# An encoder layer's feed-forward entry: one norm product of the up-projection a matmul group later, two operand steps tied behind others

## The chip, the core and the metric

The kernel runs on one core of a Trainium2 chip. The metric is the device time of one execution in microseconds (us). Engines are named as the profile names them: PE (TensorE), ACT (ScalarE), DVE (VectorE), POOL (GpSimd), SP (the engine that issues most transfers).

## What is computed

One layer of a streaming encoder over 1072 tokens (16 meta tokens and 1024 frames of a new stream, 32 frames of a running one) at width 1024: a norm, one input projection for a convolution group and for attention, an output projection with a residual, and the part that matters here:

```python
def conv_ffn(x, gate_past, g, w_up, dw_w, dw_b, w_down):
    h = rmsnorm(x, g)
    u = h @ w_up
    gate, up = u[..., :D_FF], u[..., D_FF:]
    gate_ext = jnp.concatenate([gate_past, gate], axis=1)
    y = jax.nn.silu(depthwise_causal_conv(gate_ext, dw_w, dw_b)) * up
    return x + y @ w_down, gate_ext[:, -(FFN_CONV_WIDTH - 1):]
```

`rmsnorm(x, g)` is `x / sqrt(mean(x*x) + eps) * g`, and `D_FF` is 2816: 22 row groups f of 128 channels, each with a gate row and an up row.

## The kernel before

Data lie feature by token: 128 channels on the partitions, tokens along the free dimension. A product of two float32 operands is made of three matmuls on high and low parts: high by high, high by low, low by high (`mm3`, L261). A high part is a rounded copy that ACT makes, a low part the difference, made by DVE (`hilo` for weights, L1327; `gsplit` for x times the norm's weight, L311).

Tokens come in three blocks at the end of the convolution group. `conv_half` (L1262) adds the convolution group's product to x, sums the squares of x into `rb` on POOL (L309), and makes the high and low parts `bh` and `bl` of x times the norm's weight (L312, L313). Its columns m are taken in the order 0, 1, 4, 5, 6, 7, 2, 3, so that the last low part of block 2 is that of m = 3.

The norm's scale is not applied to x but to the rows that come out of the up-projection. `rms2` (L1282) makes it for a block in three steps of `rms_steps` (L269). The first is PE's product of `rb` with ones (L280), which gives the sums over channels per token, then the mean plus eps on DVE (L283, called the variance here), its power of -1/2 on POOL (L287) and three small refining instructions on DVE (L288, L289, L291). The second is three diagonal matrices on ACT (L295). The third is PE's product of ones with the diagonals (L301), the scale broadcast to all partitions, which ACT copies to `rbg`.

The feed-forward begins with f = 0 and f = 1 in plain form. `group(f, u, p, c)` (L1676) is one product of 24 matmuls: u = 0 is the gate row and u = 1 the up row, and p and c choose one of four pieces of 264 tokens from token 16 on (268 for the first of the gate row, with its left edge). The pieces p = 0 read blocks 0 and 1 of x; group 2 of a row, the piece p = 1 and c = 0, begins at token 544 and is the first that reads block 2, which begins at token 720. The loop at L1705 makes the four groups of the gate row of f = 0, called groups 0 to 3 here. The last block's norm (`last_rms`) is put into these loops: its first step in the middle of group 1, its second behind group 1, its third behind the second group of the up row, (0, 1).

While PE works on f = 0 and f = 1, the other engines prepare f = 2, which from there on uses a scheme with seven products in place of eight (`strassen`, L1567). `t_stage` (L1450) makes sums and differences of pieces of x for it: for each of four columns j ACT makes `hraw` (L1466), DVE a chain of L1458 and L1469 in the buffer `traw`, then ACT the high part `th` (L1471) and DVE the low part `tl` (L1473, L1476), and one more sum goes to `t4`, which for p = 0 lies in the buffer of `rb`. `x_level2` (L1594) reads parts of x back: SP issues a copy of `bh` into x's buffer (L1602), and POOL an adding transfer of `bl` onto it (L1603), which needs the copy to have landed. `gate_done` (L1495) and `y_done` (L1509) apply scale, width-3 convolution and gate to a row; y_done ends with the products L1512 and L1513 and a store `yd` by SP (L1515). `w_forms` (L1367) makes the weight forms for f = 2; in it `rawr` is a pair of buffers for the third product's high and low part.

The order of PE's instructions is as written in this stage (a manual region, L1673). The other engines' instructions are put in order when the program is built, by a scheduler with its own estimates of durations; `tc.issue_after(ins)` makes what is issued in the block stand behind `ins` in its engine's list, and is no wait of itself.

Of the kernel before, what the change touches and what calls it, by code (L numbers as in the profile page):

```python
# [11 lines left out]
F32 = mybir.dt.float32  # L12
F32R = mybir.dt.float32r
AF = mybir.ActivationFunctionType
ALU = mybir.AluOpType
# [24 lines left out]
EPS = 1e-6  # L40
# [136 lines left out]
def body(nc, tc, cp, wp, xp, dp, io):  # L177
# [22 lines left out]
    def pcol(name, i):  # L200
        o, _ = PRM[name]
        return prm[:, o + i:o + i + 1]
# [38 lines left out]
    def wraw(src):  # L241
        raw = wp.tile([P, 1024], F32, tag="raw", name="raw")
        nc.sync.dma_start(raw, src)
        return raw
# [23 lines left out]
    def rms_steps(sums, c, div, R, root=False):  # L268
# [12 lines left out]
        if root:  # L281
            nc.scalar.activation(r, ss, AF.Sqrt, scale=1.0 / div, bias=eps)
        nc.vector.tensor_scalar(out=v, in0=ss, scalar1=1.0 / div, scalar2=EPS, op0=ALU.mult, op1=ALU.add)  # L283
        if root:
# [26 lines left out]
    def gsplit(hi, lo, x, g):  # L311
        nc.scalar.activation(hi, x, AF.Copy, scale=g)  # L312
        nc.vector.scalar_tensor_tensor(out=lo, in0=x, scalar=g, in1=hi.bitcast(F32), op0=ALU.mult, op1=ALU.subtract)  # L313

# [16 lines left out]
    warm = pa.tile([P, 512], F32, tag="s2", name="warm", bufs=2)  # L331
    hid, cast = {}, {}
    for i in range(WRM):
# [929 lines left out]
    def conv_half(b, rms):  # L1263
        t0, n = OB[b]
        at = t0 - H0
        for i, m in enumerate(2 * h + j for h in WOC for j in range(2)):
# [7 lines left out]
            sq_sum(X[b][:, m, :], rb[b][:, :n], acc[:, i % 4, t0:t0 + n], i, nc.gpsimd)  # L1274
            gsplit(BH[:, m, at:at + n], BL[:, m, at:at + n], X[b][:, m, :], pcol("g2", m))
            if i % 2:
# [36 lines left out]
    with tc.tile_pool(name="psB", bufs=1, space=PSUM, reuse_waits="tile") as pf:  # L1313
# [12 lines left out]

        def hilo(hi, lo, raw):  # L1327
            nc.scalar.copy(hi, raw)  # L1328
            return nc.vector.tensor_tensor(out=lo, in0=raw, in1=hi.bitcast(F32), op=ALU.subtract)

# [13 lines left out]

        def w_plain(f, u, hi, lo):
            low = hilo(hi, lo, wraw(up_src(f, u)))
            ups[f, u] = kv(hi), kv(lo)
            return low.ins
# [103 lines left out]
        def t_stage(p):  # L1452
# [9 lines left out]
            for j in range(4):  # L1462
                h, tr = hraw[j % 2][:, :n], traw[j % 3][:, 0:3 * n].rearrange("p (a b) -> p a b", a=3)
                hi, lo = THI[p][:, :, j, :], TLO[p][:, :, j, :]
                for lo_, hi_, x in x_cols(j, PAT[p], n):
                    nc.scalar.activation(h[:, lo_:hi_], x, AF.Copy, scale=pcol("g2", j))  # L1466
                less(tr[:, 0], j, PAT[p] + n, h)
                less(tr[:, 1], 4 + j, PAT[p] + n, tr[:, 0])
# [227 lines left out]
        w_plain(0, 0, *plain[:2])  # L1696
        w_plain(0, 1, *plain[2:])
        t0s, t1s = t_stage(0), t_stage(1)
# [6 lines left out]
        for i in range(4):  # L1705
            group(0, 0, i // 2, i % 2, rms_step if i == 1 else None)
            if i == 1:
                rms_step()
            next(t0s)
# [440 lines left out]
```

## Time and profile before

| | us |
|---|---|
| median of 3 runs | 1042.01 (1041.87 to 1042.07) |
| profiled execution | 1040.8 |
| its span, first to last instruction | 1038.8 |
| PE busy | 1025.8 |
| DVE busy | 871.4 |
| ACT busy | 530.7 |
| POOL busy | 192.1 |
| granted TensorE clock | 0.998 of full speed |

A row of a timeline has the start in us, the duration in us, the engine, the line, the operation, out<-in by the names of the program's tiles, shapes and a count; brackets hold how long the engine sat idle just before, and which instruction or transfer ended that. SPq is SP's issue of a transfer. Rows of one line that follow each other are merged, with their count. Instructions of an engine overlap by a few hundredths of a microsecond, so that the next may start before the last has ended.

### The profile page before, as it was taken

To read this page: it belongs to the slowest core of one execution; us is meant where nothing else is said; L and a number is where in the kernel's file an instruction comes from. 1 tells how busy PE (TensorE), PEld (TensorE's weight loads), DVE (VectorE), ACT (ScalarE), POOL (GpSimd) and SP (SyncE) were. 2 spreads that over 40 slices of the span, in tenths; PEclk is the share of its full clock that TensorE was granted. 3 is DMA by queue.
4 is the path that set the end of the run, shared out by engine and by line. 5 is a ranking of instruction groups with operands and counts; after the bars stand their busy time and mean duration, and the time that the engine had idled before them with its cause. 6 is when DMAs were issued, how large, how long until landed. Compare 5 with 4: busy or idle time off the path is not lost.

```text
span 1038.8 us, 20167 instructions
## 1 busy us (share of the span) xinstructions
PE 1025.8 (99%) x7699; PEld 999.9 (96%) x7699; DVE 871.4 (84%) x1746; ACT 530.7 (51%) x1132; POOL 192.1 (18%) x250
## 2 busy tenths in 40 slices
PE   9999999999999999999999999999999999999997
PEld 8999998868999999999999999999999999999997
DVE  7999898889887988989988988989878966986636
ACT  8654436795686654444543543544436623532334
POOL 1123220032334221021211211111100041000043
PEclk9999999999999999999999999999999999999999
DMA  7378880015853334254454445445536785832204
GB/s 270 90 166 170 173 178 21 1 43 79 156 149 118 92 80 134 84 140 145 102 141 148 117 130 155 124 124 153 152 88 229 242 178 132 266 108 80 84 1 168
DMA packets 76696, 135.35 MB, mean 130 GB/s; under 512 B 11184, under 2 KB 45608, under 8 KB 76600
## 3 DMA queue, kind: packets, MB, share of 16 engines
q1 hardware_dynamic: 58632, 100.96, 29.8%
q0 software_dynamic: 17536, 32.70, 18.6%
q8 instruction: 60, 0.98, 0.4%
q10 hardware_dynamic: 432, 0.41, 0.1%
q14 instruction: 36, 0.29, 0.1%
HBM read 81.52 MB, written 27.51 MB: 105 GB/s over the span
## 4 chain that ended last, share of the span: by engine, by line
PE 84%; DVE 6%; ACT 5%; DMA 3%; issue 2%; POOL 0%; ACTq 0%; DVEq 0%; POOLq 0%
PE mm L1441 48%; PE mm L264 8%; PE mm L265 8%; PE mm L266 8%; PE mm L1652 3%; PE S L869 1%; DMA raw<-wdn 1%; DVE x L1273 1%; DMA raw<-woc 1%; DVE bl L313 1%; PE pt L888 1%; PE o L904 1%; ACT pb L829 1%; ACT hi L353 1%; PE R L1652 1%
## 5 line engine op out<-in xcount | busy, mean ns | idle before, releaser
L1441 PE MATMUL mm<-bh,sl 128*128 128x264 f32 (+1 forms) x664 | 148.0, 284 | 0.3 <-DVE x L1588 0.3
L1441 PE MATMUL mm<-bh,wlo 128*128 128x264 f32 (+1 forms) x560 | 134.9, 285 | 0.0
L1441 PE MATMUL mm<-th,rawr 128*128 128x264 f32 x640 | 122.4, 284 | 0.0
L1441 PE MATMUL mm<-bl,sl 128*128 128x264 f32 (+1 forms) x424 | 120.4, 284 | 0.0
L1441 PEld LDWEIGHTS mm<-bh,sl 128*128 128x128 f32 x664 | 112.0, 188 | 0.6 <-DVE x L1588 0.6
L1588 DVE TENSOR_TENSOR x<-x,mm 128x264 f32<-128x264 f32 (+7 forms) x222 | 69.3, 341 | 41.6 <-PE mm L1441 41.1
L1441 PEld LDWEIGHTS mm<-th,rawr 128*128 128x128 f32 x640 | 101.5, 188 | 0.0
L1441 PEld LDWEIGHTS mm<-bh,wlo 128*128 128x128 f32 x560 | 97.6, 188 | 0.0
L264 PE MATMUL mm<-hi,whi 128*128 128x336 f32 (+3 forms) x288 | 96.0, 333 | 0.3 <-ACT hi L353 0.3
L265 PE MATMUL mm<-lo,whi 128*128 128x336 f32 (+3 forms) x288 | 93.5, 325 | 0.2 <-DVE lo L354 0.2
L266 PE MATMUL mm<-hi,wlo 128*128 128x336 f32 (+3 forms) x288 | 93.5, 325 | 0.0
L1441 PE MATMUL mm<-tl,rawr 128*128 128x264 f32 x320 | 90.9, 284 | 0.0
L1328 ACT CAST sl<-x 128x512 fp32r<-128x512 f32 (+2 forms) x66 | 40.0, 608 | 93.9 <-PE mm L1441 75.7
L1441 PE MATMUL mm<-th,sl 128*128 128x264 f32 x344 | 86.1, 285 | 0.1
L1441 PEld LDWEIGHTS mm<-bl,sl 128*128 128x128 f32 x424 | 79.7, 188 | 0.0
L1441 PE MATMUL mm<-th,wlo 128*128 128x264 f32 x272 | 77.3, 284 | 0.0
L1441 PE MATMUL mm<-tl,sl 128*128 128x264 f32 x272 | 77.2, 284 | 0.0
L1441 PE MATMUL mm<-bh,whi 128*128 128x264 f32 (+1 forms) x312 | 72.1, 285 | 0.0
L1441 PEld LDWEIGHTS mm<-th,sl 128*128 128x128 f32 x344 | 61.0, 188 | 0.3 <-ACT gx L1586 0.3
L425 DVE SCALAR_TENSOR_TENSOR acc<-glu,pdif,acc 128x545 f32<-128x545 f32 (+1 forms) x90 | 60.5, 725 | 0.1
L1441 PEld LDWEIGHTS mm<-tl,rawr 128*128 128x128 f32 x320 | 60.3, 189 | 0.0
L1441 PE MATMUL mm<-bl,whi 128*128 128x264 f32 (+1 forms) x208 | 59.2, 285 | 0.0
(494 smaller groups left out, 3169.3 us busy)
## 6 DMA issues: line engine op xcount, KB each, us to landing
x<-wup SPq DMA_DIRECT2D x48, 256.0 KB, 2.9
yq<-x SPq DMA_DIRECT2D x46, 264.0 KB, 3.0
x<-wup SPq DMA_DIRECT2D x20, 512.0 KB, 3.9
ca<-ca POOLq DMA_DIRECT2D x18, 383.0 KB, 6.7
raw<-win SPq DMA_DIRECT2D x12, 512.0 KB, 5.7
raw<-wdn SPq DMA_DIRECT2D x12, 512.0 KB, 6.3
rb<-yq SPq DMA_DIRECT2D x10, 528.0 KB, 4.5
wlo<-raw POOLq DMA_DIRECT2D x10, 512.0 KB, 5.0
```

The source lines that it names most:

```text
L264: nc.tensor.matmul(ps, whi(k), xhi(k), start=first and i == 0, stop=False)
L265: nc.tensor.matmul(ps, whi(k), xlo(k), start=False, stop=False)
L266: nc.tensor.matmul(ps, wlo(k), xhi(k), start=False, stop=last and i == n - 1)
L313: nc.vector.scalar_tensor_tensor(out=lo, in0=x, scalar=g, in1=hi.bitcast(F32), op0=ALU.mult, op1=ALU.subtract)
L353: hid[b, k] = nc.scalar.activation(HI[b][:, k, :], X[b][:, k, :], AF.Copy, scale=pcol("g1", k)).ins
L425: nc.vector.scalar_tensor_tensor(out=out, in0=x, scalar=w, in1=into, op0=ALU.mult, op1=ALU.add)
L829: nc.scalar.activation(qs_[i], qs_[i], AF.Exp, bias=m[0][:, i:i + 1], scale=-1.0, accum_out=m[1][:, i:i + 1])
L869: nc.tensor.matmul(S2[kv][:, j, 0:n], q, kT[ks, self.at:self.at + n], start=True, stop=True)
L1328: nc.scalar.copy(hi, raw)
L1441: nc.tensor.matmul(ps, w[:, j, :], x[:, j, :], start=first and j + i == 0, stop=j == 3 and i == 2, skip_group_check=True)
L1588: summed[0] = nc.vector.tensor_tensor(out=z, in0=z, in1=ps[:, lo_:hi_], op=ALU.add).ins
L1652: nc.tensor.matmul(ps, z[:, j, :], x[:, j, :], start=q in FIRST and j + i == 0, stop=j == 1 and i == 2, skip_group_check=True)
```

## The change

Three things are edited. The last block's sums (the product L280, with its second step behind the group) go from group 1 to group 2 of the first row. The low part of the weight (0, 1) gets an order behind x's last low part. And in the first `t_stage`, the first DVE sum of column j = 2 gets an order behind x's last low part, that of column j = 3 one behind the variance. Nothing else is computed, added or left out.

```diff
-        nc.vector.tensor_scalar(out=v, in0=ss, scalar1=1.0 / div, scalar2=EPS, op0=ALU.mult, op1=ALU.add)
+        var = nc.vector.tensor_scalar(out=v, in0=ss, scalar1=1.0 / div, scalar2=EPS, op0=ALU.mult, op1=ALU.add)
+        ended["var"] = var.ins
...
-            gsplit(BH[:, m, at:at + n], BL[:, m, at:at + n], X[b][:, m, :], pcol("g2", m))
+            low = gsplit(BH[:, m, at:at + n], BL[:, m, at:at + n], X[b][:, m, :], pcol("g2", m))
+            ended["bl"] = low.ins
...
-        def hilo(hi, lo, raw):
+        def hilo(hi, lo, raw, behind=None):
             nc.scalar.copy(hi, raw)
-            return nc.vector.tensor_tensor(out=lo, in0=raw, in1=hi.bitcast(F32), op=ALU.subtract)
+            with tc.issue_after(behind) if behind else nullcontext():
+                return nc.vector.tensor_tensor(out=lo, in0=raw, in1=hi.bitcast(F32), op=ALU.subtract)
...
-        def w_plain(f, u, hi, lo):
-            low = hilo(hi, lo, wraw(up_src(f, u)))
+        def w_plain(f, u, hi, lo, behind=None):
+            low = hilo(hi, lo, wraw(up_src(f, u)), behind)
...
-                less(tr[:, 0], j, PAT[p] + n, h)
+                with tc.issue_after(ended["bl" if j == 2 else "var"]) if p == 0 and j > 1 else nullcontext():
+                    less(tr[:, 0], j, PAT[p] + n, h)
...
-        w_plain(0, 1, *plain[2:])
+        w_plain(0, 1, *plain[2:], ended["bl"])
...
         for i in range(4):
-            group(0, 0, i // 2, i % 2, rms_step if i == 1 else None)
-            if i == 1:
+            group(0, 0, i // 2, i % 2, rms_step if i == 2 else None)
+            if i == 2:
                 rms_step()
             next(t0s)
```

The lists of instructions differ between these groups and the end of f = 0's y_done; from there on they are the same, and SP's is the same throughout. Line numbers of the changed kernel are 1 to 4 higher. PE's list differs only by the sums' place. The three places below are where the other lists differ most for what follows. In the names a number tells buffers apart: `traw_3683` and `traw_3681` hold the third and the fourth column's sums of the first `t_stage`, `traw_3682` one of the second, and `x_2345` and `x_2344` are the buffers of x's blocks 1 and 0, which are reused as scratch.

DVE before, from the fourth column's last sum to the first refining instruction (L288) behind the variance (L283):

```order
L1469 TENSOR_TENSOR traw_3681<-traw_3681,hraw_3685 128x264
L1473 TENSOR_TENSOR tl_3675<-traw_3683,th_3673 128x3x264
L1458 SCALAR_TENSOR_TENSOR rb<-x_2344,prm,traw_3683 128x264
L283 TENSOR_SCALAR stat<-R 128x3
L1458 SCALAR_TENSOR_TENSOR rb<-x_2344,prm,traw_3681 128x264
L1476 TENSOR_TENSOR tl_3675<-traw_3681,th_3673 128x3x264
L1458 SCALAR_TENSOR_TENSOR traw_3682<-x_2346,prm,hraw_3685 128x264
L288 SCALAR_TENSOR_TENSOR stat<-stat 128x3
```

DVE after, from the third column's last sum to the same refining instruction, now L289:

```order
L1473 TENSOR_TENSOR traw_3683<-traw_3683,hraw_3684 128x264
L1477 TENSOR_TENSOR tl_3675<-traw_3683,th_3673 128x3x264
L1461 SCALAR_TENSOR_TENSOR rb<-x_2344,prm,traw_3683 128x264
L283 TENSOR_SCALAR stat<-R 128x3
L1461 SCALAR_TENSOR_TENSOR traw_3681<-x_2344,prm,hraw_3685 128x56
L1461 SCALAR_TENSOR_TENSOR traw_3681<-x_2345,prm,hraw_3685 128x208
L1461 SCALAR_TENSOR_TENSOR traw_3681<-x_2344,prm,traw_3681 128x56
L1461 SCALAR_TENSOR_TENSOR traw_3681<-x_2345,prm,traw_3681 128x208
L289 SCALAR_TENSOR_TENSOR stat<-stat 128x3
```

The fourth column's sums went behind the variance, and its last sum, its part of t4 and its low part went behind the first refining instruction.

POOL before, around the power (`stat<-stat,mhalf`):

```order
L1493 COPY gx_3677<-prm 128x2
L287 TENSOR_TENSOR stat<-stat,mhalf 128x3
L1603 DMA x_2345<-bl 128x2x268
L1493 COPY x_2346<-prm 128x2
L1603 DMA x_2345<-bl 128x2x268
```

POOL after, the same instructions:

```order
L1497 COPY gx_3677<-prm 128x2
L1607 DMA x_2345<-bl 128x2x268
L288 TENSOR_TENSOR stat<-stat,mhalf 128x3
L1497 COPY x_2346<-prm 128x2
L1607 DMA x_2345<-bl 128x2x268
```

The first adding transfer of x_level2 went ahead of the power.

DVE before, from the gate's last taps (L1503) of f = 0 past the low part of the weight (1, 1) to y_done's products L1512 and L1513:

```order
L1503 SCALAR_TENSOR_TENSOR x_2344<-gx_3677,prm,x_2344 128x1058 x2
L1329 TENSOR_TENSOR wlo<-raw,whi 128x1024
L1607 TENSOR_TENSOR x_2345<-x_2345 128x4
L1507 TENSOR_TENSOR x_2344<-x_2344,rbg 128x1058
L1608 TENSOR_TENSOR x_2345<-x_2345 128x4
L1512 TENSOR_TENSOR x_2344<-x_2344 128x1024
L1513 TENSOR_TENSOR x_2344<-x_2344 128x32
```

DVE after, from that low part on; the gate's last tap is L1507 there, y_done's products are L1516 and L1517:

```order
L1332 TENSOR_TENSOR wlo<-raw,whi 128x1024
L1611 TENSOR_TENSOR x_2345<-x_2345 128x4
L1507 SCALAR_TENSOR_TENSOR x_2344<-gx_3677,prm,x_2344 128x1058
L1612 TENSOR_TENSOR x_2345<-x_2345 128x4
L1613 TENSOR_TENSOR x_2345<-x_2345 128x4
L1614 TENSOR_TENSOR x_2345<-x_2345 128x268
L1615 TENSOR_TENSOR x_2345<-x_2345 128x268
L1511 TENSOR_TENSOR x_2344<-x_2344,rbg 128x1058
L1616 TENSOR_TENSOR x_2345<-x_2345 128x268
L1620 TENSOR_TENSOR x_2345<-x_2345 128x268
L1516 TENSOR_TENSOR x_2344<-x_2344 128x1024
L1517 TENSOR_TENSOR x_2344<-x_2344 128x32
```

The last tap went behind the weight's low part, and the four sums of 268 columns of x_level2 (L1614 to L1616 and L1620) went ahead of y_done's products.

More of the change, by code (lines that the diff above doesn't have):

```diff
@@ L312, in gsplit @@
         nc.scalar.activation(hi, x, AF.Copy, scale=g)
-        nc.vector.scalar_tensor_tensor(out=lo, in0=x, scalar=g, in1=hi.bitcast(F32), op0=ALU.mult, op1=ALU.subtract)
+        return nc.vector.scalar_tensor_tensor(out=lo, in0=x, scalar=g, in1=hi.bitcast(F32), op0=ALU.mult, op1=ALU.subtract)
     diag = [cp.tile([P, P], F32, tag=f"diag{i}", name=f"diag{i}") for i in range(4)]
@@ L331, in body @@
     warm = pa.tile([P, 512], F32, tag="s2", name="warm", bufs=2)
-    hid, cast = {}, {}
+    hid, cast, ended = {}, {}, {}
     for i in range(WRM):
```

## The prediction

> **What bounds the kernel now.** The page's first part says which engine sets the time.
>
> ```profile
> span 1038.8 us, 20167 instructions
> PE 1025.8 (99%) x7699; PEld 999.9 (96%) x7699; DVE 871.4 (84%) x1746; ACT 530.7 (51%) x1132; POOL 192.1 (18%) x250
> ```
>
> TensorE is busy for 1025.8 of 1038.8 us, so a change of order can win only idle time of PE, 13.0 us in all, and it loses wherever it makes PE wait. The second view is PE's timeline through the stage that the change touches, with the idle time before a row in brackets.
>
> ```profile
> 342.04 0.28 PE L266 MATMUL mm<-bh,wlo 128*128 128x264 f32 x1
> 343.89 0.83 PE L280 MATMUL R<-ones,rb 128*128 128x1 f32 x6 [1.57 <-POOL rb L309]
> 344.58 0.37 PE L264 MATMUL mm<-bh,whi 128*128 128x264 f32 x1
> ...
> 357.81 0.83 PE L301 MATMUL R<-diag,ones 128*128 128x128 f32 x6
> 358.40 0.37 PE L264 MATMUL mm<-bh,whi 128*128 128x264 f32 x1
> ...
> 373.43 0.28 PE L266 MATMUL mm<-bh,wlo 128*128 128x264 f32 x1
> ...
> 393.88 0.40 PE L1441 MATMUL mm<-th,rawr 128*128 128x264 f32 x2
> ...
> 405.33 0.28 PE L1441 MATMUL mm<-bh,sl 128*128 128x264 f32 x1
> ```
>
> The one bracket is the wait that the change aims at: the sum product of the last norm (L280, "the sums" from here on) stands in the middle of group 1 and needs rb, which GpSimd finishes at 343.85. Five groups of 24 matmuls lie between 358.40 and the third matmul of the sixth at 373.43, so a matmul starts every 0.123 us (15.03 over 122), and without the wait the row of 343.89 would start at 342.16: 1.73 us are there to win. From 344 to 405 PE never waits; whatever the new order delays has to stay ahead of these rows.
>
> The third view is the timeline of the other engines, for how far ahead they are. First the path from the sums to the broadcast product of L301.
>
> ```profile
> 347.11 0.61 DVE L1458 SCALAR_TENSOR_TENSOR traw<-x,prm,traw 128x56 f32<-128x56 f32 x2
> ...
> 349.07 0.42 DVE L1469 TENSOR_TENSOR traw<-traw,hraw 128x264 f32<-128x264 f32 x1
> 350.41 0.98 DVE L1473 TENSOR_TENSOR tl<-traw,th 128x792 fp32r<-128x792 f32 x1
> 351.72 0.15 DVE L283 TENSOR_SCALAR stat<-R 128x3 f32<-128x3 f32 x1
> 353.49 0.15 DVE L288 SCALAR_TENSOR_TENSOR stat<-stat 128x3 f32<-128x3 f32 x1
> ```
> ```profile
> 349.52 0.86 ACT L1471 CAST th<-traw 128x792 fp32r<-128x792 f32 x1 [3.60 <-DVE traw L1469]
> 350.28 0.70 ACT L1466 ACTIVATE hraw<-x,prm 128x176 f32<-128x176 f32 x2
> 356.66 0.97 ACT L295 ACTIVATE diag<-ident,stat 128x128 f32<-128x128 f32 x3
> ```
> ```profile
> 351.95 1.04 POOL L287 TENSOR_TENSOR stat<-stat,mhalf 128x3 f32<-128x3 f32 x1 [7.78 <-DVE stat L283]
> 353.96 1.25 POOL L1603 DMA_DIRECT2D x<-bl  x1 [0.97 <-DMA x<-bh]
> ...
> 390.64 2.44 POOL L1603 DMA_DIRECT2D x<-bl  x2 [4.23 <-DMA x<-bh]
> ```
> ```profile
> L1603 POOL DMA_DIRECT2D x<-bl x4: 1205/1236/1667, 354.0 to 391.4; - x4
> ```
> ```profile
> 350.75 0.67 SPq L1602 DMA_DIRECT2D x<-bh  x1
> ...
> 374.31 0.33 SPq L1515 DMA_DIRECT2D yd<-x  x1
> 387.31 1.52 SPq L1602 DMA_DIRECT2D x<-bh  x2
> ```
>
> Read them together: variance at 351.72 (L283), power on GpSimd at 351.95, the three diagonals end at 356.66 + 0.97 = 357.63, and PE takes them at 357.81, so this path has 0.2 us to spare. GpSimd's next instruction, the adding transfer x<-bl, had to wait for x<-bh to land, 353.96 - 350.75 = 3.21 us after its issue; the later pair took 390.64 - 387.31 = 3.33. The last row (nanoseconds of the shortest, median and longest issue; first and last start) says that after an issue at 390.64 the next began at 391.4.
>
> **The change part by part.** The profiled execution took 1040.8 us against a span of 1038.8; the median of the runs shown is 1042.01. I work in shifts against the trace and add them to the median.
>
> *The sums a group later.* PE runs from 342.16 through the second half of group 1 and the first half of group 2: 24 x 0.123 = 2.95 us, so it meets the sums at 345.1. rb is there since 343.85. Gain 1.73, and PE would meet L301 at 357.81 - 1.73 = 356.1. But group 2 is the first to read x's last block: its eleventh matmul needs the last low part of x (L313) at 342.16 + 22 x 0.123 = 344.9.
>
> ```profile
> 344.05 1.21 DVE L1329 TENSOR_TENSOR wlo<-raw,whi 128x1024 fp32r<-128x1024 f32 x1
> ...
> 345.72 0.58 DVE L313 SCALAR_TENSOR_TENSOR bl<-x,prm,bh 128x352 fp32r<-128x352 f32 x1
> ```
>
> *The weight's low part behind it.* As it stands that low part ends at 346.30, too late by 1.4. The tie swaps them: L313 from 344.05 to 344.63, 0.2 us early, the weight's L1329 to 345.8. Its reader, group (0,1), starts at about 350.1 and the raw tile that it frees is refilled 0.5 later for use at 370: both cost nothing.
>
> *The tie behind the variance, and what it moves.* The lists show three consequences. First, DVE's L1469 of x's third sum now ends at 349.06 with nothing between it and the tl that needs ACT's cast of it, so DVE waits 0.9 there and the variance comes at 351.3, 0.4 earlier than before. Second, the fourth sum's four instructions (L1458) stand behind the variance. Third, on GpSimd the power has gone behind the transfer x<-bl. That transfer waits for x<-bh, whose issue follows ACT's hraw (0.47 us after the row of 350.28); hraw starts 0.43 earlier, so x<-bh is issued at 350.3, lands at 350.3 + 3.21 = 353.5, and the power starts when x<-bl is issued: 0.76 later as between the two issues of 390.64 and 391.4, or 1.25 by the row of 353.96. I take 1.0, so the power's 1.04 ends at about 355.6 instead of 352.99. SP's list is the same as before, and DVE's tail and ACT's move only inside this stage.
>
> The variance and the fourth sum's two pairs, 1.1 us together by the row of 347.11, bring DVE to the first statistics instruction (L288 before, L289 after) at 352.4. There it stands until 355.65, 3.2 us, and everything in its list stands behind it. The next of them, L1469 of the fourth sum, ends at 356.15; ACT's cast and two hraw stand ahead of the diagonals (0.76 from 349.52 to 350.28, and 0.6 for the pair, 0.70 less its overlap), so these start at 357.5. For PE waiting on diagonals there is one case in the trace:
>
> ```profile
> 43.81 0.98 ACT L295 ACTIVATE diag<-ident,stat 128x128 f32<-128x128 f32 x3 [3.69 <-DVE stat L291]
> ```
> ```profile
> 44.26 1.07 PE L301 MATMUL R<-diag,ones 128*128 128x128 f32 x6
> 45.09 0.41 PE L264 MATMUL mm<-hi,whi 128*128 128x352 f32 x1
> ```
>
> The group resumes 45.09 - 43.81 = 1.28 after the diagonals start: 358.8 instead of 358.40. So PE waits some 1.7 us at L301 where it never waited, and the gain of 1.73 is a loss of 0.4.
>
> *The lag of DVE.* The question is what DVE is late for next.
>
> ```profile
> 358.41 0.98 DVE L1473 TENSOR_TENSOR tl<-traw,th 128x792 fp32r<-128x792 f32 x1 [0.77 <-ACT th L1471]
> ...
> 370.37 1.22 DVE L1329 TENSOR_TENSOR wlo<-raw,whi 128x1024 fp32r<-128x1024 f32 x1
> ...
> 374.05 0.18 DVE L1513 TENSOR_TENSOR x<-x 128x32 f32<-128x32 f32 x1
> 374.34 0.44 DVE L1610 TENSOR_TENSOR x<-x 128x268 f32<-128x268 f32 x1
> ...
> 378.89 1.26 DVE L1329 TENSOR_TENSOR bl<-t,bh 128x1056 fp32r<-128x1056 f32 x1 [2.83 <-ACT bh L1328]
> ...
> 390.64 0.68 DVE L1329 TENSOR_TENSOR rawr<-x,rawr 128x512 fp32r<-128x512 f32 x1
> ...
> 403.23 0.42 DVE L1588 TENSOR_TENSOR rb<-rb,mm 128x264 f32<-128x264 f32 x1
> ```
> ```profile
> 377.11 0.38 ACT L1690 COPY x<-mm 128x264 f32<-128x264 f32 x1 [3.34 <-DMA yd<-x]
> 377.78 1.08 ACT L1328 CAST bh<-t 128x1056 fp32r<-128x1056 f32 x1 [0.30 <-PE mm L266]
> ```
>
> The weight's low part of 370.37 ends at 371.59, 1.8 before PE's row of 373.43 reads it. In the new list it follows all of the t sums and two gate taps; adding the steps from 355.65 it ends at about 373.8 to 374.1, against PE's 373.43 + 0.4: a stall of 0 to 0.3.
>
> The first gate row's last product (L1513) ends at 374.23, 20.74 us after L288 started. In the new list more stands between the two: one L1469 (0.42), one t4 sum like L1458's (0.48), one tl (0.98), one t sum (0.48) and four sums of L1610's kind (0.44 each), 4.1 together, about 3.5 since neighbours overlap by 0.08; the idle 0.77 before 358.41 gets covered, and waits for ACT put back 0.5. So 355.65 + 20.74 + 3.2 = 379.6, 5.4 late. Its store yd is issued from SP then, and ACT's copy of 377.11, in whose place the next row's product goes, waits for the store's landing: 377.11 - 374.23 = 2.88 after L1513, so 382.5. ACT's cast bh (at least 0.29 behind the copy) starts at 382.8 instead of 377.78, DVE's bl 1.11 later at 383.9 instead of 378.89; the 2.83 idle there becomes some 4.4. From there the weight forms of f = 2 come in the old order: rawr (390.64) follows bl by 11.75, so it starts at 395.6 and ends at 396.3. It is the low part of f = 2's third product, whose third matmul is PE's row of 393.88. Before it was 2.5 us early; now PE, by itself at 393.88 + 0.4 to 0.6, waits for it some 1.9 us.
>
> *The sum.* L301 +0.4, the weight of (1,1) +0.15, rawr about +1.85: PE goes on at 396.3 where it stood at 393.88, +2.4 us. Span 1038.8 to 1041.2, median 1042.01 to 1044.4, slower by 0.23%. The unknown is when the power runs: x<-bl's issue of 0.76 to 1.67 (the longest of the four) and a landing of 3.21 to 3.33 move the sum from +2.1 to +3.2; the middle of the two usual issues gives +2.4.
>
> [...]
>
> **The rivals.** *B, faster.* If x<-bh had landed when GpSimd gets there, power and diagonals would run 0.4 earlier than before, PE would not wait at L301, and 1.73 would be won there. Against it speak the two waits of 0.97 and 4.23 in GpSimd's rows. DVE would still be late by the list: L1513 at 352.5 + 24.0 = 376.5, rawr's end at 393.2 against PE's 393.88 - 1.73 = 392.15, a stall of 1.0. Net -0.7: 1041.3. It decides if x<-bh lands before 351.5, 1.2 us after issue.
>
> *C, the gain is only given back.* The late power holds PE at L301, but the row store or the forms of f = 2 have more slack than I add up (2.5 us in the trace): +0.4, 1042.4. Against it: between 358 and 379 DVE has no idle to catch up in but the 0.77 already counted.
>
> *D, the lag goes on.* In f = 2 PE's seventh product (row of 405.33) accumulates in the bank that DVE's L1588 of 403.23 empties, 1.7 us ahead. DVE would be 5.0 us late there and PE 2.4; if DVE has made up nothing, that is another wait of 2.6 - 1.7 = 0.9: +3.3, 1045.3.
>
> That the change doesn't do what it says is excluded by the lists: the sums stand in group 2, and both ties hold.
>
> **How the numbers follow.** My case has 0.64, of which 0.10 lies under +2.08 us; B 0.17, C 0.10, D 0.08, and 0.01 is left for a gain over 2.08, which the one stall cannot pay. About 0.2%, 2.08 us, is what a measurement of this kernel can tell from no change. Slower: 0.54 + 0.08 = 0.62. Same: 0.10 + 0.17 + 0.10 = 0.37. Faster: 0.01. My case's own range is 1044.0 to 1045.2; the range given reaches down to B and up to D.
>
> **What would show it.** In the profile of the changed kernel: no wait before the sums on PE; a wait of about 1.7 before L302 (L301 before), released by ACT's diagonals; on GpSimd x<-bl ahead of the power with a wait for x<-bh; on DVE about 3.2 us before L289, released by GpSimd; on ACT over 5 us before a copy x<-mm, released by yd; on PE a wait near 394 for DVE's rawr. Were the power done by 353, or PE without a wait at 394, I am wrong.

## The result

The changed kernel takes 1045.92 us, the median of six executions from 1044.87 to 1048.55; the kernel before, run beside it, 1041.0 (six, 1039.3 to 1042.07). The ratio is 1.0053, with a 95% interval of 1.0036 to 1.0071. A second measurement, beside other runs of the kernel before, gave 1.0042 (1.0027 to 1.0058). The change makes the kernel slower, by 4.4 to 5.5 us by these ratios and by 4.9 and 5.0 between the medians, where 2.4 were forecast. The direction and the chain of causes up to the first row's store were as predicted; what that store's landing took, and a second wait behind the first, were not. (Two executions at a far lower granted clock are left out everywhere, one of the kernel before at 1671.65 us and 0.557 of full speed and one of b5 at 1242.67 us and 0.753.)

The profiled execution of the changed kernel took 1047.91 us:

```profile
span 1045.9 us, 20166 instructions
PE 1027.9 (98%) x7699; PEld 1000.7 (96%) x7699; DVE 871.8 (83%) x1746; ACT 530.0 (51%) x1132; POOL 192.6 (18%) x250
```

Medians of the kernel before lie between 1041.0 and 1042.8, and the traces differ by up to 1.4 us at the point where the change begins. So this document measures a **stretch** in each trace: from TensorE's first 268-column matmul of group 0 of the first gate row to the second 268-column matmul of a product of f = 4. (The expectations below count from the same row to that product's first matmul, 0.12 us less throughout.) In the kernel before:

```profile
337.66 0.37 PE L264 MATMUL mm<-bh,whi 128*128 128x268 f32 x1
...
449.27 0.29 PE L1441 MATMUL mm<-bl,sl 128*128 128x268 f32 x1
```

That is 111.61 us. In the changed kernel, PE's timeline with the sums, its five waits and the end of the stretch:

```profile
338.39 0.37 PE L264 MATMUL mm<-bh,whi 128*128 128x268 f32 x1
345.96 0.72 PE L280 MATMUL R<-ones,rb 128*128 128x1 f32 x6
359.03 1.07 PE L302 MATMUL R<-diag,ones 128*128 128x128 f32 x6 [2.05 <-ACT diag L296]
390.48 0.40 PE L1444 MATMUL mm<-bh,sl 128*128 128x268 f32 x1 [0.95 <-ACT sl L1330]
392.12 0.52 PE L1444 MATMUL mm<-bh,sl 128*128 128x268 f32 x2 [1.12 <-DVE sl L1332]
400.06 0.51 PE L1444 MATMUL mm<-th,rawr 128*128 128x264 f32 x2 [1.84 <-DVE rawr L1332]
412.59 0.39 PE L1444 MATMUL mm<-bh,sl 128*128 128x264 f32 x1 [0.81 <-DVE rb L1592]
456.63 0.29 PE L1444 MATMUL mm<-bl,sl 128*128 128x268 f32 x1
```

The stretch is 118.24 us, 6.63 longer. The sums' wait of 1.57 is gone, and five others, 6.77 together, have come: 2.05 for the diagonals and 4.72 inside f = 2. (A wait costs more than its bracket: the last matmul before L302 started at 356.70, so 2.33 us lie between the starts where 0.12 would.) The engines behind them, POOL and SP first, then DVE and ACT:

```profile
354.49 1.24 POOL L1607 DMA_DIRECT2D x<-bl  x1 [9.39 <-DMA x<-bh]
355.29 1.37 POOL L288 TENSOR_TENSOR stat<-stat,mhalf 128x3 f32<-128x3 f32 x1
```
```profile
351.27 0.67 SPq L1606 DMA_DIRECT2D x<-bh  x1
380.91 0.33 SPq L1519 DMA_DIRECT2D yd<-x  x1
```
```profile
356.69 0.16 DVE L289 SCALAR_TENSOR_TENSOR stat<-stat 128x3 f32<-128x3 f32 x1 [3.24 <-POOL stat L288]
380.65 0.18 DVE L1517 TENSOR_TENSOR x<-x 128x32 f32<-128x32 f32 x1
```
```profile
358.60 0.97 ACT L296 ACTIVATE diag<-ident,stat 128x128 f32<-128x128 f32 x3
386.18 0.38 ACT L1694 COPY x<-mm 128x264 f32<-128x264 f32 x1 [7.68 <-DMA yd<-x]
```

All the signs that the prediction named are here: no wait before the sums; a wait before L302 released by the diagonals; the power behind x<-bl, which waits for x<-bh (354.49 - 351.27 = 3.22 after its issue); DVE standing 3.24 before L289; over 5 us before the copy x<-mm, released by the row's store yd; and PE waiting for rawr, at 400.06 where about 394 was named. What is new is in the last row: the copy comes 386.18 - 380.91 = 5.27 us after the store's issue, where before it was 377.11 - 374.31 = 2.80. The view of the DMA queues from 381.0 to 386.2, in 40 slices of 0.13 us, shows why it is long:

```profile
DMA  0000058899897993000000200100000000000000
GB/s 0 0 0 0 0 227 357 357 455 422 357 422 292 455 548 130 0 0 0 0 0 0 32 0 0 32 0 32 32 0 32 32 32 32 0 0 0 0 0 0
...
q1 hardware_dynamic: 144, 0.54, 25.9%
q8 instruction: 1, 0.02, 1.1%
```

The store is 128 packets of 4 KB. For 1.4 us they move at some 400 GB/s, with the 16 DMA engines mostly 0.7 to 0.9 busy; then nothing for 0.8 us, and then single packets at 32 GB/s, one after another. Between lies one 16 KB packet of the queue named instruction, which starts at 382.94 and takes 0.96 by the packet records. I read it as TensorE's next instructions and call it the fetch: the queue's 60 packets in the whole program are one for every 257 of TensorE's 15398 matmuls and weight loads. 120 of the 128 packets have ended 2.27 us after the issue, as in the kernel before (2.17). The eight that are left are a sixteenth of the store, which I take for the share of one of the 16 DMA engines; the packet records name no engine. The last eight begin when the fetch ends, 2.97 us after the issue, and end at 4.66, before at 2.26. No other packet moved in this time.

### The profile page after: what moved, and what is told of

Read it like the earlier page. It is cut to its first block, busy times and chain, and to the rows that moved or that the text cites. A ratio compares the mean times of both kernels' runs of the same rounds, so it can differ in the third digit from the quotient of the medians.

```text
span 1045.9 us, 20166 instructions
## 1 busy us (share of the span) xinstructions
PE 1027.9 (98%) x7699; PEld 1000.7 (96%) x7699; DVE 871.8 (83%) x1746; ACT 530.0 (51%) x1132; POOL 192.6 (18%) x250
## 4 chain that ended last, share of the span: by engine, by line
PE 78%; DVE 9%; ACT 6%; DMA 4%; issue 3%; POOL 1%; ACTq 0%; DVEq 0%; POOLq 0%; SPq 0%
PE mm L1444 46%; PE mm L264 7%; PE mm L266 7%; PE mm L265 7%; PE mm L1656 3%; PE S L870 1%; DMA raw<-wdn 1%; DVE traw L1461 1%; DMA raw<-woc 1%; DVE bl L314 1%; PE pt L889 1%; PE o L905 1%; DVE x L1274 1%; ACT pb L830 1%; DMA x<-wup 1%
## 5 line engine op out<-in xcount | busy, mean ns | idle before, releaser
L1592 DVE TENSOR_TENSOR x<-x,mm 128x264 f32<-128x264 f32 (+7 forms) x222 | 69.2, 341 | 40.1 <-PE mm L1444 39.5
```

Of the source, the lines that this page charges most:

```text
L1592: summed[0] = nc.vector.tensor_tensor(out=z, in0=z, in1=ps[:, lo_:hi_], op=ALU.add).ins
```

## The experiments

**The theories.** Theory 1, the prediction's: the power stands behind x<-bl on GpSimd, DVE waits 3.2 us for it, the first gate row is late, and all that follows it in DVE's chain is late for TensorE. Rival 1: DVE's new order costs, whatever the power does. Rival 2: the loss sits at L302 and right behind it, not in the row's store. Theory 3, formed on the trace above: the instruction fetch falls among the store's packets and holds the last eight of them back, some 2.4 us. Each ratio compares 5 to 12 executions with those of the kernel before that were run beside them (13 to 27, and six in the changed kernel's first measurement), with a 95% interval; it is not the ratio of the two medians, which differs from it by up to 0.0009.

| kernel | time against before | stretch, us | store's issue to the copy | fetch starts after the issue |
|---|---|---|---|---|
| before | | 111.61 | 2.80 | 6.02 |
| changed | 1.0053 (1.0036 to 1.0071) | 118.24 | 5.27 | 2.03 |
| a2 changed again | 1.0042 (1.0027 to 1.0058) | 115.10 | 2.79 | 2.67 |
| a3, a4, a5, one execution each | | 118.11, 117.73, 117.93 | 5.22, 5.07, 4.59 | 1.40, 1.11, 1.06 |
| e1 power first | 1.0003 (0.9993 to 1.0013) | 112.87 | 3.03 | 2.39 |
| e4 ties alone | 1.0006 (0.9994 to 1.0019) | 111.31 | 2.79 | 3.58 |
| e3 sums alone | 1.0026 (1.0017 to 1.0036) | 114.12 | no wait for it | 8.61 |
| n1 row store elsewhere | 1.0010 (0.9998 to 1.0022) | 112.23 | no wait for it | |
| p24 24 small matmuls more | 1.0083 (1.0068 to 1.0099) | 119.72 | no wait for it | 3.50 |
| w1, w2, w3: 1, 2, 3 wide matmuls more | 1.0032, 1.0030, 1.0032 | 116.39, 115.16, 116.38 | 3.36, 2.80, 2.81 | 2.72, 2.49, 4.58 |
| b4 all amended | 0.9973 (0.9965 to 0.9982) | 109.89 | 2.79 | 4.67 |
| b5 as b4, power behind | 1.0008 (0.9996 to 1.0019) | 112.47 | 2.80 | 4.42 |

(The intervals of w1, w2 and w3: 1.0021 to 1.0043, 1.0019 to 1.0041, 1.0019 to 1.0044.)

### e1: the power ahead of the transfer

```diff
-            nc.gpsimd.tensor_tensor(out=r, in0=v, in1=mhalf[:, :ns], op=ALU.pow)
+            ended["pow"] = nc.gpsimd.tensor_tensor(out=r, in0=v, in1=mhalf[:, :ns], op=ALU.pow).ins
...
-                    nc.gpsimd.dma_start(st[:, i], l2_blocks(BL, 4 + r + 2 * i), accum_op=ALU.add)
+                    with tc.issue_after(ended["pow"]) if r + i == 0 else nullcontext(): nc.gpsimd.dma_start(st[:, i], l2_blocks(BL, 4 + r + 2 * i), accum_op=ALU.add)
```

> The changed kernel, and the transfer x<-bl is tied behind the power, so that GpSimd's list is that of the kernel before; every other list is that of the changed kernel. Theory 1 (the power behind the transfer holds VectorE 3.2 us, and everything after it is late for that): the wait before L289 on VectorE is under 0.5 us, TensorE doesn't wait at L302, the first gate row is done near 377.5 instead of 380.8, and, if its store lands in about 2.9 us as it did before, the time is 1.1 us below the kernel before (1040); if the store takes 5.3 again, 1.3 above it (1042.3). Rival 1 (the new order of VectorE's list costs, whatever the power does): still about 5 us above the kernel before (1046).

Against the changed kernel two instructions of GpSimd's list have changed places, and nothing else. POOL, ACT and PE:

```profile
352.33 0.86 POOL L288 TENSOR_TENSOR stat<-stat,mhalf 128x3 f32<-128x3 f32 x1 [7.38 <-DVE stat L283]
354.35 1.25 POOL L1607 DMA_DIRECT2D x<-bl  x1 [1.16 <-DMA x<-bh]
```
```profile
380.59 0.38 ACT L1694 COPY x<-mm 128x264 f32<-128x264 f32 x1 [5.45 <-DMA yd<-x]
```
```profile
394.46 0.51 PE L1444 MATMUL mm<-th,rawr 128*128 128x264 f32 x2 [1.55 <-DVE rawr L1332]
407.06 0.39 PE L1444 MATMUL mm<-bh,sl 128*128 128x264 f32 x1 [0.88 <-DVE rb L1592]
```

The power waits for the variance alone, DVE doesn't wait before L289 nor PE at L302, and the stretch is 5.4 us shorter than the changed kernel's: the power's place is the head of the chain, and Rival 1 falls as the whole account. DVE's new order has a price of its own, though: this is still 1.26 longer than before with the 1.70 at the sums won, and b4 below takes that away. My figure was still 2.4 too low (1.1 below the kernel before; measured 1.26 longer in the stretch, 1.0003 in time). The gain at the sums is whole: from the stretch's start to the first 268-column matmul of f = 1, TensorE needs 30.84 us instead of 32.54. But the row's store goes out 39.33 us after the start of the stretch instead of 36.65, 2.7 late, while PE comes 1.7 early, and PE waits 1.55 and 0.88 in f = 2.

### e4: the two ties alone

```diff
-            group(0, 0, i // 2, i % 2, rms_step if i == 2 else None)
-            if i == 2:
+            group(0, 0, i // 2, i % 2, rms_step if i == 1 else None)
+            if i == 1:
```

> The changed kernel with the sums put back into the middle of group 1, so the two ties alone; GpSimd's list is that of the kernel before, power ahead of the transfer. Theory 1: no wait at L302, the first gate row done near 377 (2.5 us later than before), which the slack of f=2's forms just covers: within 0.3 us of the kernel before (1041). Rival 1 (the ties' order on VectorE is what costs): 2 to 5 us above the kernel before.

1.0006 and a stretch 0.30 shorter than before, with 0.73 us of wait left before the sums and 0.28 at L1592. The ties alone cost nothing that shows, though the row's store goes out 1.7 late (38.35 after the stretch's start).

### e3: the sums alone

```diff
-                with tc.issue_after(ended["bl" if j == 2 else "var"]) if p == 0 and j > 1 else nullcontext():
+                with nullcontext():
...
-        w_plain(0, 1, *plain[2:], ended["bl"])
+        w_plain(0, 1, *plain[2:])
```

> The sums a group later without the two ties: the weight's low part and the sums of x keep the order that the scheduler gives them. On GpSimd the power still stands behind the transfer x<-bl. Theory 1: the last low part of x comes 1.2 us late for group 2, and the diagonals stand behind the weight's cast on ScalarE, so TensorE waits 2 to 4 us at L302; the first gate row is done as early as before, so there is no wait near 390 to 412. The stretch takes about 113.3 us against 111.5 before, the time 1 to 2 us above the kernel before. Rival 1 (the moved sums themselves delay everything, the ties are harmless): as slow as the changed kernel, 118 us.

```profile
347.19 0.39 PE L265 MATMUL mm<-bl,whi 128*128 128x264 f32 x1 [1.53 <-DVE bl L314]
360.71 1.07 PE L302 MATMUL R<-diag,ones 128*128 128x128 f32 x6 [2.15 <-ACT diag L296]
```

As expected: two waits, none in f = 2, 2.51 longer than before in the stretch and 1.0026 in time. So moving the sums without the first tie costs 1.53 at the last low part, and moving them at all puts the power behind the transfer. The row's store is on time here (36.68 after the stretch's start), since DVE has other work to do before L289. The ties make it late, by 1.7 in e4 and 2.7 in e1, and the power behind the transfer adds 3.2 to that in the changed kernel.

### n1: nothing waits for the row's store

```diff
-                nc.sync.dma_start(yd[f][:, NMETA:T], Y[:, NMETA:T])
+                nc.sync.dma_start(yd[f][:, NMETA:T], (Y if f else rbg)[:, NMETA:T])
```

> The changed kernel, but the store of the first gate row takes its data from the tile rbg, of the same size, so that nothing waits for that store (the stored first row is thereby not the gated row; the rest is computed as before). Theory 1 with the store's landing as the mis-sized term: the copy x<-mm follows the row's product at about 381 instead of 386.2, TensorE's waits near 390 to 400 shrink from 3.9 us to under 0.5, and the time is 0.2 to 1.0 us above the kernel before (1041.2 to 1042). Rival 2 (the loss sits in the wait at L302 and in what VectorE has to do after it, not in the store): at least 4 us above the kernel before.

```profile
358.11 1.07 PE L302 MATMUL R<-diag,ones 128*128 128x128 f32 x6 [1.60 <-ACT diag L296]
```
```profile
380.15 0.38 ACT L1694 COPY x<-mm 128x264 f32<-128x264 f32 x1 [2.35 <-DVE x L1517]
```

The copy now follows DVE's product. That PE row is the only wait of the stretch, which is 6.0 us shorter than the changed kernel's and 0.62 longer than before's; in time 1.0010. The product is as late as in the changed kernel (it ends 42.14 after the stretch's start, there 42.44), but without the store's landing behind it the lag doesn't reach TensorE. Rival 2 falls: L302 by itself costs what the gain at the sums brings, and 0.62 more.

### p24 and w1: moving the fetch, first tries

```diff
         w11 = w_plain(1, 1, *plain[2:])
+        for i in range(24): nc.tensor.matmul(ended['R'][:, 480:481], ones, ones[:, 0:1], start=True, stop=True)
```

(`ended['R']` is the tile R of the last norm. For w1 the added line is a single `nc.tensor.matmul(ended['R'], ones, rbg[:, NMETA:NMETA + 512], start=True, stop=True)`.)

> The changed kernel with 24 one-column matmuls more on TensorE between the last group of f=0 and the first of f=1 (results not read; they cost 24 x 0.12 = 2.9 us of TensorE and are 96 instructions). The other engines' lists are unchanged. TensorE's next 16 KB of instructions are then fetched about 2.9 us earlier against the work (near 380.0 instead of 382.94), ahead of the packets of the row store. Theory 3 (the fetch sits on one of the 16 DMA engines in the way of the store's last share): the store's issue to its use takes 2.9 us instead of 5.3, the waits near 390 to 400 are under 0.5 us instead of 3.9, and the time is 0.5 to 1.5 us below the changed kernel although TensorE has 2.9 us more to do. Rival (the store is slow for another reason): it takes 5.3 again, about 1 us of the waits is left, and the time is that of the changed kernel.

```profile
364.80 5.74 PE L1723 MATMUL R<-ones 128*128 128x1 f32 x48
```

The price was twice the expected one: 5.74 us, not 2.9, or 0.06 us for each of the 96 matmuls and weight loads, as in the groups (0.123 for a pair), so by my estimate the fetch moved little against the work (it began 3.50 us after the issue), and PE was late enough that nothing waited for the store. The granted clock also fell to 0.50, from the last of these matmuls on (369.72 to 376.55). The time says nothing about Theory 3. The store itself had no fetch among its packets, and its last packet ended 2.27 after the issue.

> The changed kernel with one 512-column matmul more on TensorE between the last group of f=0 and the first of f=1 (its result is not read; about 1.4 us by the 0.18 us of a 128-column pass at L302). All other engines keep the changed kernel's lists. TensorE then reaches its next fetch of instructions about 1.2 us later, behind the packets of the row store instead of among them. Theory 3 (the fetch on one DMA engine delays the store's last share): issue to use 2.9 us instead of 5.3, and the stretch from the first 268-column matmul to the one near 449 takes 116 us, 2 less than in the changed kernel, although TensorE has 1.4 us more to do there. Rival (the store is slow for another reason, or isn't what holds TensorE): 5.3 us again and 118 us or more.

Between the two: 3.36 us to the copy, the last packet at 2.71, and a stretch 1.85 shorter than the changed kernel's although PE had 0.85 us more to do. It points to Theory 3, but the effect is not whole, and a wait of 1.81 at rawr was followed by a fall of the granted clock (0.70 from 395 to 400 us), which adds to this stretch.

### a2 to a5: the changed kernel again

> The changed kernel once more, unedited, for its time beside the runs of the kernel before on the same chip and for a second trace. Measured from TensorE's first 268-column matmul of group (0,0) to the first one of the last 268-column product near 449 us, the stretch took 111.5 us in the trace of the kernel before and 118.1 in that of the changed one. If the 5.3 us from the row store's issue to its use belong to this order (TensorE's instruction fetch meets the store at the same point of the program each time): again about 5.3, and about 118 us. If that was an accident of one execution: about 2.9, and about 115.7 us.

> The changed kernel unedited, a third trace, to see how often the row store meets the instruction fetch. Theory 3: with a fetch starting within about 2.3 us of the store's issue the store takes over 3.3 us to its use and the stretch 117 us or more; with a later fetch 2.8 us and 115 us. A fall of the granted clock after the wait at L302 is hidden if VectorE's chain is what TensorE waits for near 397 to 412 anyway.

> The changed kernel unedited, a fourth trace; as for the third: over 3.3 us and 117 us or more with a fetch that starts within about 2.3 us of the issue, else 2.8 us and 115 us.

> The changed kernel unedited, a fifth trace; as for the third: over 3.3 us and 117 us or more with a fetch that starts within about 2.3 us of the issue, else 2.8 us and 115 us.

Four of the five traces have the long store, and those four take 117.7 to 118.2 us in the stretch; the fifth, a2, has the short one and takes 115.10. In all four, the store's last eight packets begin within 0.02 us of the end of the fetch. The granted clock fell to 0.50 for 3.4 us in a3 and a4, behind the waits at sl (its mean from 390 to 395 us is 0.78 and 0.70, from 395 to 400 0.87 and 0.96), and in a5, behind the wait at rawr (0.94 from 395 to 400 us, 0.72 from 400 to 405), but not in the first trace, whose stretch is the longest: where it fell, smaller waits followed (0.30 and 0.28 at rawr in a3 and a4, where the first trace has 1.84). The third trace and a2, SP and ACT:

```profile
381.60 0.33 SPq L1519 DMA_DIRECT2D yd<-x  x1
...
386.82 0.38 ACT L1694 COPY x<-mm 128x264 f32<-128x264 f32 x1 [7.64 <-DMA yd<-x]
```
```profile
380.16 0.33 SPq L1519 DMA_DIRECT2D yd<-x  x1
```

What made a2 different is in the table by stages of PE (time, PE busy, granted clock, DMA share, GB/s), from 355 to 365 us:

```profile
355.00:360.00 5.00, 2.96 (x20) 0.86 0.37 55
360.00:365.00 5.00, 5.00 (x35) 0.80 0.04 11
```

After the wait at L302 the clock fell, matmuls started 0.22 us apart instead of 0.123 until 362, and PE came 1.4 us later. The fetch begins, in each trace of the table that has one, when 5001 to 5023 of TensorE's matmuls and weight loads have started, so with PE late it came 2.67 after the store's issue, behind its packets. The later PE cost nothing here, since it was going to wait for DVE in f = 2 anyway (0.41 and 0.38 were left).

### w2 and w3: the fetch behind the store

As w1, with `for i in range(2)` and `range(3)` ahead of the wide matmul.

> As w1, with two 512-column matmuls (0.85 us each by w1's trace, 1.7 us of TensorE more than the changed kernel). In the four traces of the changed kernel in which the row store was slow, the fetch started 1.06 to 2.03 us after the store's issue; here it should start 2.8 to 3.7 after it, behind the store's packets. Theory 3: 2.8 us from the store's issue to its use, and 115.0 us for the stretch from the first 268-column matmul to the one near 449, as in the one trace of the changed kernel where the fetch came late, 2.8 less than in the other four (117.6 to 118.1), although TensorE has 1.7 us more to do. Rival: 4.6 to 5.3 us again, and 118 us or more.

> As w1, with three 512-column matmuls (2.55 us of TensorE). The fetch should start 3.6 to 4.6 us after the store's issue. Theory 3: 2.8 us to the store's use, and 115 to 115.5 us for the stretch: VectorE's chain sets it, and the added matmuls take the place of TensorE's waits. Rival (the added matmuls simply add): 120 us.

In w2, SP's and ACT's rows, the DMA queues from 380.7 to 385.9, and PE's waits:

```profile
380.70 0.33 SPq L1519 DMA_DIRECT2D yd<-x  x1
...
383.50 0.38 ACT L1694 COPY x<-mm 128x264 f32<-128x264 f32 x1 [5.20 <-DMA yd<-x]
```
```profile
GB/s 0 0 0 0 0 0 357 390 455 325 487 455 357 455 357 487 33 0 0 126 0 0 0 0 0 0 0 0 0 0 0 0 0 0 0 0 0 0 0 0
```
```profile
359.03 1.07 PE L302 MATMUL R<-diag,ones 128*128 128x128 f32 x6 [2.03 <-ACT diag L296]
...
397.36 0.51 PE L1444 MATMUL mm<-th,rawr 128*128 128x264 f32 x2 [0.15 <-DVE rawr L1332]
...
409.43 0.39 PE L1444 MATMUL mm<-bh,sl 128*128 128x264 f32 x1 [0.34 <-DVE rb L1592]
```

The fetch is the lone slice of 126 GB/s, after the store's last packet. The store takes 2.80 us again, the tail of 32 GB/s is gone, and the stretch is 115.16: 3.1 less than in the changed kernel's first trace, with 1.7 us more work on TensorE and every other engine's list unchanged. That is Theory 3's case, in one trace each of w2 and w3. The fetch came 2.49 after the issue, where 2.8 to 3.7 was expected: the added work moved it by 0.5 to 1.4 us against the four traces with the long store, and a2 shows that it moves as much without an edit. What carries Theory 3 is both together, the order of the packets in every trace and the store's time here. The times don't show it: 1.0030 to 1.0032, with intervals that overlap those of the changed kernel. In w3 the store takes 2.81, and the stretch 116.38, 0.9 to 1.4 over the expectation: after the wait at L302 the clock fell again (0.73 from 360 to 365 us), and this time, with 2.55 us of added work, nothing was left to hide it.

### b4 and b5: a version that keeps the gain

b4 is e1 with three ties more: the weight's low part of (1,1) behind the row's last convolution step, and x_level2's sums and the last t low part of p = 1 behind the row's last product (`ended["g"]` and `ended[0]` are set where these two are issued):

```diff
-                    nc.vector.tensor_tensor(out=lo, in0=tr, in1=hi.bitcast(F32), op=ALU.subtract)
+                    with tc.issue_after(ended[0]) if p else nullcontext(): nc.vector.tensor_tensor(out=lo, in0=tr, in1=hi.bitcast(F32), op=ALU.subtract)
...
-                tt_(out=h, in0=h, in1=b21[:, 0:e], op=ALU.subtract)
+                with tc.issue_after(ended[0]): tt_(out=h, in0=h, in1=b21[:, 0:e], op=ALU.subtract)
...
-        w11 = w_plain(1, 1, *plain[2:])
+        w11 = w_plain(1, 1, *plain[2:], ended["g"])
```

> The changed kernel with the power ahead of x<-bl, and VectorE's list amended: the last t low part of p=1 and the sums of the second transform behind the first gate row's last product, the weight's low part of (1,1) behind the row's last convolution step, so that the row is done about 3 us earlier than in e1. Theory 1: no wait of TensorE at L302 nor near 390 to 407 (e1 had 1.55 and 0.88 there), so the 1.7 us of the old wait before the sums stay won: the stretch takes 109.8 us against 111.5 before, and the time is 1.7 us below the kernel before. Rival 1 (VectorE's later list has other costs that then show): 111.5 us or more, no better than before.

```profile
338.06 0.37 PE L264 MATMUL mm<-bh,whi 128*128 128x268 f32 x1
...
447.95 0.29 PE L1444 MATMUL mm<-bl,sl 128*128 128x268 f32 x1
```
```profile
352.15 0.86 POOL L288 TENSOR_TENSOR stat<-stat,mhalf 128x3 f32<-128x3 f32 x1 [7.37 <-DVE stat L283]
```
```profile
377.24 0.38 ACT L1694 COPY x<-mm 128x264 f32<-128x264 f32 x1 [4.66 <-DMA yd<-x]
```

No wait of PE is left in the stretch: 109.89 us, 1.72 less than before. The time is 1039.68 (1038.76 to 1040.42 over 12 executions) against 1041.75, a ratio of 0.9973 (0.9965 to 0.9982): faster than both kernels. Moving the sums was worth its 1.7 us; what came with the move took it away. Against e1 the stretch is 2.98 shorter: most of that is what DVE's new order cost there.

> The last version (VectorE's list amended) with the power behind x<-bl again, as in the changed kernel: the two differ in the order of two instructions on GpSimd alone. Theory 1: TensorE waits about 2 us at L302 and nowhere else in the stretch, since the row is 3 us earlier than in the changed kernel: the stretch takes 112.2 us (111.5 before, less 1.7, plus 2.4 with the resumption), 2.4 more than with the power ahead; the time is 0.5 to 2 us above the kernel before, more where the granted clock falls after the wait as it did in the second trace of the changed kernel (1.4 us). Rival 4 (with the row early, the power's place no longer matters): 109.8 us and the time of the last version.

```profile
358.60 1.07 PE L302 MATMUL R<-diag,ones 128*128 128x128 f32 x6 [1.65 <-ACT diag L296]
...
374.93 0.39 PE L266 MATMUL mm<-bh,wlo 128*128 128x264 f32 x1 [0.32 <-DVE wlo L1332]
```

112.47, where 112.3 by this document's count was expected, and 2.58 more than b4: the price of two instructions in the wrong order on GpSimd, with no wait behind them in f = 2. In time 1.0008.

## Why the prediction was right and wrong

**Right: the gain and the power.** The 1.73 us at the sums are there to within 0.03 where nothing spoils them (e1: 1.70; b4: 1.72). The power behind the transfer, DVE's 3.2 us (3.24) and the diagonals came as worked out. Taking off the 0.73 us that this execution was late at the stretch's start, the diagonals start at 357.87 (357.5 forecast) and the first part of the stretch is 0.74 longer than before, where a loss of 0.4 was forecast: the power itself took 1.37 instead of 1.04. The stall of 0 to 0.3 at the weight of (1,1) did not come.

**Nearly right: the row's lateness.** L1513, now L1517, was forecast 5.4 late; the store's issue is 42.52 after the stretch's start instead of 36.65, 5.87 late.

**Wrong: the size of the store's landing.** The step that failed is the term "ACT's copy of 377.11 ... waits for the store's landing: 377.11 - 374.23 = 2.88 after L1513, so 382.5". It took one duration from the one trace that showed it. In four of the five traces of the new order the store goes out 1.06 to 2.03 us ahead of the next fetch, and there it took 4.6 to 5.3 us. From 2.80 to 5.27 these are 2.5 us in a chain without slack, and nearly all of them arrive at rawr. The forecast was that PE goes on there 2.4 late. Counted from the stretch's start it is 2.74 late in a2 and 2.75 in w2, where the store takes 2.8, and 5.45, 5.46, 5.16 and 4.68 in the first trace, a3, a4 and a5, where it takes 5.27, 5.22, 5.07 and 4.59. So with the short store the forecast's sum up to rawr is off by 0.35, and with the long one by 2.3 to 3.1.

**Wrong: leaving out rival D.** The sum ended at rawr. Behind it the stretch loses 0.75 more in a2, 0.80 in w2 and 1.18 in the first trace, most of it the wait for L1588's add, now L1592, that rival D put at 0.9 (its sum: +3.3, 1045.3) and that I gave a chance of 0.08. The wait is there in the rows: 0.81 in the changed kernel, 0.38 in a2, 0.34 in w2, 0.88 in e1. The evidence stood in the prediction: 1.7 us of slack there against 2.5 at rawr. A lag of 5 us that meets both goes by the smaller one, unless DVE catches up between, and it hardly does. In a2, whose stretch starts 0.20 later than that of the kernel before (there the two rows start at 390.64 and 403.23):

```profile
396.09 0.68 DVE L1332 TENSOR_TENSOR rawr<-x,rawr 128x512 fp32r<-128x512 f32 x1
...
408.46 0.42 DVE L1592 TENSOR_TENSOR rb<-rb,mm 128x264 f32<-128x264 f32 x1
```

DVE is 5.25 late at rawr and 5.03 at the add. It does idle between the two, 3.3 us before and 3.0 in a2, but waiting for ACT, so it makes up 0.2. D's condition, that DVE makes up nothing, thus held to within 0.2 us, and no row in the prediction spoke against it: a chance of 0.08 was too little.

**Rivals B and C.** B needed x<-bh to land 1.2 us after its issue; it took 3.22. C, that the late power only eats the gain, is what n1 (0.62 longer) and b5 (0.86) show where the row's store holds nothing up: the mechanism existed, but not its condition.

**What stays open.** The medians show 4.9 and 5.0 us, the four traces with the long store 6.1 to 6.6, the one with the short store 3.5. A mix of both among the changed kernel's executions would fit, but only five of them have a trace. The clock of the kernel before plays in as well: its trace has no fall before the program's end, while of its 27 executions beside e1 the 11 with a mean clock of 0.999 took 1040.9 us on average and the eight with 0.996 or 0.997 took 1044.0. Where those lose it, no trace shows; the wait of 1.57 at the sums is shorter than waits that cost no clock in other traces (1.65 in b5).

## What to carry over

Before moving a product, look where its consumers' small steps land in the other engines' lists: here the scheduler put a one-microsecond step behind a transfer whose wait holds it, and DVE stood 3.24 us for it, with everything behind it in its list. When a lag of several microseconds runs through a chain, list every reader with its own slack and take the smallest, not the first that comes to mind. And a transfer's duration in one trace need not be its duration in another: from issue to use this store took 2.80 us before and 4.59 to 5.27 in four of the five traces of the changed kernel.

## What the runs showed of the hardware

**A store's last packets behind an instruction packet.** In the traces of the kernel before and of the changed one the queue q8, named instruction, moves 60 packets of 16 KB, singly and 12 to 23 us apart (364.96, 380.32 and 398.17 in the kernel before), and each takes 0.9 to 1.8 us. When one started 1.06 to 2.03 us after the issue of a 528 KB store, among that store's packets (the changed kernel's first trace, a3, a4, a5), the store's last packet ended 3.98 to 4.66 us after the issue; when it started 3.5 us or more after (the kernel before, e3, e4, p24, w3, b4, b5), 2.26 to 2.28; between 2.39 and 2.72 (e1, a2, w1, w2), 2.26 to 2.71. What came late in the changed kernel's first trace is eight of the store's 128 packets, while the other 120 had ended 2.27 us after the issue. No wait of PE in the stretch is for such a packet. The cost that the rows show falls on a store behind which ACT stands: the copy comes 4.59 to 5.27 us after the issue where it was 2.80, so 1.8 to 2.5 us later.

**A wait of 2 us cost clock in some traces.** After PE's wait at L302, 2.03 to 2.15 us long, the granted clock fell in a2 (wait of 2.04) and w3 (2.07) and stayed at 1.00 in the other traces with such a wait, among them the changed kernel's first (2.05), w2 (2.03) and e3 (2.15). From 355 to 360 and from 360 to 365 us its mean is 0.86 and 0.80 in a2 and 0.93 and 0.73 in w3, which is about 3.4 us at 0.50. The wait at rawr shows the same: 1.81 us in w1, where the clock fell (0.70 from 395 to 400 us), and 1.84 in the changed kernel's first trace, where it didn't. In e1, n1 and b5, whose longest waits are 1.55, 1.60 and 1.65, it stayed at 1.00 from 335 to 450 us. (The fall in p24, 0.50 from 370 to 375 us, came in its one-column matmuls and not behind a wait.) So the length of one wait doesn't tell whether the clock falls behind it, and what does, no run here was made to show.
